# Linear attention: state products one chunk in advance, normed rows turned two levels on, 48 projections in front of the first scores

## The chip, the cores and the metric

The kernel runs on one core of one Trainium2 chip. A core has TensorE (PE, matrix products and transposes into PSUM), VectorE (DVE), ScalarE (ACT), GpSimd (POOL) and SyncE (SP, which issues DMAs); each works through a queue of its own, in order, and waits for the others at semaphores. The metric is the device time of the whole program in microseconds (us), as the median of several runs; lower is better.

## What is computed

One layer on 1024 tokens of width 1024, in fp32: a mixer of two kinds of gated linear attention (four heads with keys of 128, and four heads with keys of 64), an output projection with a norm, and a mixture of 64 experts, two for each token, with a second norm. The change is in the mixer. Cut to what matters:

```python
def chunk_gla(q, k, v, log_g):                       # per head; b = cumulative sum of log_g
    decay = jnp.exp(jnp.where(causal, diff, -jnp.inf))
    scores = jnp.einsum('bhntsk,bhnsk->bhnts', q[..., :, None, :] * decay, k)
    o_intra = jnp.einsum('bhnts,bhnsv->bhntv', scores, v)
    u = jnp.einsum('bhnsk,bhnsv->bhnkv', k * jnp.exp(b_last - b), v)
    def step(S, inp):                                # the running state, chunk after chunk
        g_n, u_n = inp
        return g_n[..., None] * S + u_n, S
    ...
    o_inter = jnp.einsum('bhntk,bhnkv->bhntv', q * jnp.exp(b), s_prev)
    o = o_intra + o_inter

def hybrid_mixer(x, w_in, w_a2, b_a, lb, norm_h, norm_g, w_out):
    hq, hf, hi, hg, gq, gk, gv, ga, gg = jnp.split(x @ w_in, split_at, axis=-1)
    ...
    o_h = head_rms_norm(o_h, norm_h) * jax.nn.silu(hg.astype(jnp.float32))
    ...
    o_g = head_rms_norm(o_g, norm_g) * jax.nn.silu(gg.astype(jnp.float32))
    o = jnp.concatenate([o_h, o_g], axis=-1).astype(x.dtype)
    return o @ w_out
```

The experts' weights, 64 times three matrices of 1024 x 512, are 403 MB; each is read from HBM once.

## The kernel before

**The two parts.** First the mixer with its output projection and the router, then the experts, whose weights stream through SBUF in tiles of 2 MB. The first four of these tiles are loaded while the output projection runs; the rest begins when the router has finished.

**Order.** TensorE's order is the order of the code (`tc.manual_schedule` for PE). The queues of VectorE, ScalarE and GpSimd are put in order by the scheduler of the language, from what the code issues; so a change of TensorE's code also moves instructions on those.

**Projections.** `queue` lists the blocks of `x @ w_in`, each 128 columns wide, with what is done to its result. A block is 48 products of 128 x 512 (L176, L178 and L180: x and the weights are split into a high and a low part of fp32r, three products make one) in two halves of 24; its weights are loaded, cast on ScalarE (L155, `wh`) and subtracted on VectorE (L156, `wl`). `fill(n)` issues the next n products of the queue; the mixer uses them to cover the other work. `to_rows` takes a block of values: ScalarE copies a half to SBUF (L217, `vt`), TensorE transposes it some projections later (L222; `late` holds the count at which), and VectorE copies it to `VOA` (L223). `gated` multiplies `VOA` by a silu gate (L229, L231).

**Units.** `gla(u, ...)` runs for units 0 to 5: units 0 to 3 are one head each, units 4 and 5 two heads of half width. A unit works on chunks of 128 tokens (`NT` = 8). Its scores are made in seven levels: `level` builds decayed keys and queries (GpSimd L471 and L472 subtract cumulative sums, ScalarE L473 takes the exponential, VectorE L436, or L454 with two heads, and L475 multiply into `K2` and `Qb`, two buffers each), `scores` makes the products (TensorE L485, then L500, and L512 or L518), and VectorE masks them into `acc` (L422, L424). For each level: `fill(n_lv)`, one of the turns left by the unit before, then the scores. A turn (L616) transposes half a head of normed rows, which VectorE scales first (L610, after a chain of small operations on the squares' sums, L80 to L88), and VectorE copies the result to `VOA` (L617).

**Chunks.** Behind the levels comes a loop over the chunks. The output of chunk c is q times the running state (L576) plus scores times values (L578); the state's own product (L584) follows, and VectorE updates the state in one of the two tiles `Sg` (L591 copies the first, L593 does the others). ScalarE sums the squares of the output (L598), VectorE copies it to `osb` (L599). Then comes one step of the next unit's preparation (gates, the scans L393, on VectorE, ScalarE and GpSimd), and `fill(n_ch)`. Outputs and state products share the PSUM pool `ps_ou`, three buffers; a new tile gets the buffer that was released first in the program's order. Turns, transposes and scores share `ps_tr`, two buffers.

Of the kernel before, what the change touches and what calls it, by code (L numbers as in the profile page):

```python
# [9 lines left out]
F32 = mybir.dt.float32  # L10
# [4 lines left out]
OP = mybir.AluOpType  # L15
# [5 lines left out]
NT = T // 128  # L21
# [35 lines left out]
def mixer_moe_kernel(ctx: ExitStack, tc: tile.TileContext, x_in, xT_in, wf_in, wv_in, wvg_in, wa2_in,  # L57
# [3 lines left out]
    V, S, G, PE = nc.vector, nc.scalar, nc.gpsimd, nc.tensor  # L61
# [8 lines left out]
    VOA = voap.tile([128, NT, NH, 128], F32, name="VOA")  # L70
# [33 lines left out]
    ps_ou = psA.enter_context(tc.tile_pool(name="ps_ou", bufs=3, space=PSUM))  # L104
# [27 lines left out]
    Sg = [pers.tile([128, 256], F32, name=f"Sg{i}") for i in range(2)]  # L132
# [3 lines left out]
    queue, wts, late = [], {}, []  # L136
    done, count, cur, limit = [0], [0], [None], [0]
# [63 lines left out]
    def fill(n):  # L201
        end = count[0] + n
        while count[0] < end and step():
            pass
# [8 lines left out]
    def to_rows(h):  # L213

        def evac(ps, ts):
            vt = g2.tile([128, 512], F32, name="vt", bufs=1)
            S.copy(vt, ps)  # L217

            def turn():
                tp = ps_tr.tile([128, 4, 128], F32, name="trp")  # L220
                for i in range(4):
                    PE.transpose(tp[:, i], vt[:, i * 128:(i + 1) * 128], ident)  # L222
                V.tensor_copy(VOA[:, ts.start // 128:ts.stop // 128, h], tp)  # L223
            late.append((count[0] + 10, turn))
        return evac

    def gated(h):
# [166 lines left out]
            if c % 2:  # L394
                yield

    def gla(u, n_lv, n_ch, before, during):


        h0, nh, sc = (u, 1, 1.0) if u < 4 else (2 * u - 4, 2, 1.0 / 16.0)  # L400
        q, k, lg, P = ready.pop(u)
        dk = 128 // nh
        W = nh * 128
        Pc = P.rearrange("p (c i) -> p c i", i=128)
        A = Ab
        KLt = g1.tile([128, NT, 128], F32, name="KLt")
# [118 lines left out]
        QI = g1.tile([128, T], F32, name="QI")  # L525
        gdec = small.tile([128, NT], F32, name="gdec")
# [19 lines left out]
            S.copy(KLt[:, half * 4:half * 4 + 4], tp)  # L546

        kqs = {0: level(0)}
        for li in range(7):
            if li < 6:  # L550
                kqs[li + 1] = level(li + 1)
            if li == 2:
                decayed_k()
            if li == 3:
                decayed_q()
            fill(n_lv)
            if before:
                before.pop(0)()
            if li in (5, 6):
                turn_k(li - 5)  # L560
            scores(li, *kqs.pop(li))
# [6 lines left out]
        if u < 5:  # L568
            need(at[f"q{u + 1}"])
        steps = during()  # L570
        Sp = None
        for c in range(NT):
            cs = slice(c * 128, (c + 1) * 128)
            op = ps_ou.tile([128, W], F32, name="ou")
            if c:
                PE.matmul(op, QI[:, cs], Sp[:, :W], start=True, stop=False)  # L576
            for hh in range(nh):
                PE.matmul(op[:, hh * 128:(hh + 1) * 128], A[hh][:, c], VOA[:, c, h0 + hh], start=(c == 0),  # L578
                          stop=(c == 0 or hh == nh - 1))
            if c < NT - 1:  # L580
                up = ps_ou.tile([128, 128], F32, name="ou")
                for hh in range(nh):
                    r = slice(hh * dk, (hh + 1) * dk)
                    PE.matmul(up[r], KLt[:, c, r], VOA[:, c, h0 + hh], start=True, stop=True)  # L584
                gcol = gdec[:, c:c + 1]
                Sn = Sg[c % 2]
                for hh in range(nh):
                    r = slice(hh * dk, (hh + 1) * dk)
                    w = slice(hh * 128, (hh + 1) * 128)
                    if c == 0:  # L590
                        V.tensor_copy(Sn[r, w], up[r])  # L591
                    else:
                        V.scalar_tensor_tensor(Sn[r, w], Sp[r, w], gcol[r], up[r], op0=OP.mult, op1=OP.add)  # L593
                Sp = Sn
            for hh in range(nh):
                w = slice(hh * 128, (hh + 1) * 128)
                junk = small.tile([128, 128], BF, name="junk")
                S.activation(junk, op[:, w], AF.Square, accum_out=ssq[hh][:, c:c + 1])  # L598
                V.tensor_copy(osb[hh][:, c], op[:, w])  # L599
            next(steps, None)  # L600
            fill(n_ch)
# [4 lines left out]
        turns = []  # L606
# [14 lines left out]
    def mixer():  # L621
        limit[0] = at["g6"]
        for i in range(8):
            PE.matmul(zp, zt[:, 0:128], zt, start=True, stop=True)
        first_blocks()
        setup()
        for _ in prepare(0):
            pass
        turns = []
        for u in range(6):  # L630
            turns = gla(u, 18 if u == 0 else 12, 12 if u < 5 else 6, turns, (lambda: prepare(u + 1)) if u < 5 else (lambda: iter(())))
        for t_ in turns:
            t_()
        limit[0] = len(queue)

    with tc.manual_schedule(engines={mybir.EngineType.PE}):
        mixer()
        gl.close()
# [14 lines left out]
    gcol = tb.tile([128, NE // 2], F32, name="gcol")  # L653
# [711 lines left out]
```

## Time and profile before

| | us |
|---|---|
| median of 3 runs | 1620.42 |
| lowest to highest | 1619.65 to 1620.74 |
| the profiled execution | 1625.67 |
| its span, first to last instruction | 1623.8 |
| TensorE busy | 1447.7 |
| VectorE busy | 726.0 |
| ScalarE busy | 404.4 |
| GpSimd busy | 272.0 |

The mean granted clock of TensorE is 0.957 of its full speed. The profile cuts the span into 40 slices of 40.6 us. Slices 0 to 11 are the mixer, 12 to 15 the output projection and the router, 16 to 39 the experts. A busy time says how long an engine works, a list of waits who it waited for, a timeline what stands in its queue and what ended an idle time before an instruction (in square brackets).

### The profile page before, as it was taken

How to read it: one execution, taken by the hardware profiler on the slowest of the kernel's cores; microseconds unless marked ns; L12 is line 12 of the kernel's file. 1: busy time of each engine (PE TensorE's matmuls, PEld its weight loads, DVE VectorE, ACT ScalarE, POOL GpSimd, SP SyncE). 2: the span in 40 equal slices, each digit the busy share in tenths (PEclk: the TensorE clock that was granted, in tenths of full speed). 3: DMA queues.
4: the chain of work that ended last, by engine and by line, in shares of the span. 5: the costliest groups of instructions: out<-in, count | busy, mean ns of one | idle time of the engine just before them, and what ended most of it. 6: DMA issues, size and time to landing. Idle time of an engine off the chain costs nothing. (4 is left out here: it accounts for less than half of the span.)

```text
span 1623.8 us, 22905 instructions
## 1 busy us (share of the span) xinstructions
PE 1447.7 (89%) x9303; PEld 809.3 (50%) x9303; DVE 726.0 (45%) x1842; ACT 404.4 (25%) x749; POOL 272.0 (17%) x228
## 2 busy tenths in 40 slices
PE   7899899999999997999989989989988989988985
PEld 5677677777778775334334333333333433333432
DVE  4656544666856995233323322422422422422424
ACT  5345443435543232211111110110110110110110
POOL 4523231423202552010000000000000000000000
PEclk9899999899999997999999999999999999999998
DMA  4111100010117316999999999999999999999992
GB/s 164 34 33 34 34 27 27 27 41 20 35 46 309 125 61 255 393 425 425 427 425 427 426 425 427 426 426 426 426 427 426 426 426 426 425 427 426 423 393 89
DMA packets 61966, 450.18 MB, mean 277 GB/s; under 512 B 12192, under 2 KB 20640, under 8 KB 36896
## 3 DMA queue, kind: packets, MB, share of 16 engines
q1 hardware_dynamic: 50768, 430.01, 63.8%
q0 software_dynamic: 9216, 12.61, 2.2%
q10 hardware_dynamic: 1872, 6.06, 1.0%
q8 instruction: 74, 1.21, 0.3%
q14 instruction: 36, 0.29, 0.1%
HBM read 448.63 MB, written 20.97 MB: 289 GB/s over the span
## 5 line engine op out<-in xcount | busy, mean ns | idle before, releaser
L1150 PE MATMUL gu<-w2u,VOA 128*64 128x512 f32 x1024 | 253.8, 625 | 49.8 <-DMA w2u<-in_wu_dram 34.6
L1150 PE MATMUL gu<-w1u,VOA 128*64 128x512 f32 x1024 | 258.2, 623 | 36.8 <-DMA w1u<-in_wu_dram 27.6
L1026 DVE TENSOR_TENSOR sg<-sg,gu 128x512 f32<-128x512 f32 x32 | 22.0, 688 | 543.5 <-PE gu L1150 543.5
L1150 PEld LDWEIGHTS gu<-w1u,VOA 128*64 128x64 f32 x1024 | 84.6, 144 | 205.3 <-issue 148.6
L1150 PEld LDWEIGHTS gu<-w2u,VOA 128*64 128x64 f32 x1024 | 80.5, 144 | 213.0 <-issue 143.1
L176 PE MATMUL pp<-xh,wh 128*128 128x512 f32 x416 | 177.7, 427 | 0.0
L178 PE MATMUL pp<-xl,wh 128*128 128x512 f32 x416 | 167.1, 402 | 0.5 <-issue 0.5
L180 PE MATMUL pp<-xh,wl 128*128 128x512 f32 x416 | 167.4, 402 | 0.0
L1009 POOL DMA_INDIRECT out_dram<-VOA,oidx x32 | 32.3, 1008 | 604.9 <-DVE VOA L1051 593.1
L1036 ACT COPY hT<-tp 128x512 f32<-128x512 f32 x32 | 18.8, 586 | 394.1 <-PE tp L1034 394.1
L1176 PE MATMUL yp<-w1u,hT 128*64 128x512 f32 x512 | 116.4, 595 | 0.0
L1176 PE MATMUL yp<-w2u,hT 128*64 128x512 f32 x512 | 113.4, 595 | 0.0
L1042 ACT ACTIVATE y<-yp,gcol 128x512 fp32r<-128x512 f32 x64 | 44.0, 688 | 190.1 <-PE yp L1176 190.1
L176 PEld LDWEIGHTS pp<-xh,wh 128*128 128x128 f32 x416 | 81.0, 195 | 18.6 <-issue 2.4
L180 PEld LDWEIGHTS pp<-xh,wl 128*128 128x128 f32 x416 | 80.5, 194 | 18.6
L178 PEld LDWEIGHTS pp<-xl,wh 128*128 128x128 f32 x416 | 81.2, 195 | 15.0 <-issue 0.8
L471 POOL TENSOR_TENSOR d<-P 128x512 f32<-128x512 f32 x36 | 47.9, 1331 | 229.2 <-DVE Qb L475 152.7
L1043 DVE SCALAR_TENSOR_TENSOR y<-yp,gcol,y 128x512 fp32r<-128x512 f32 x64 | 47.9, 749 | 76.5 <-ACT y L1042 76.3
L1004 POOL DMA_INDIRECT VOA<-x1d,gidx x32 | 32.8, 1024 | 290.2 <-issue 214.3
L1025 ACT ACTIVATE sg<-gu 128x512 f32<-128x512 f32 x32 | 19.1, 597 | 240.0 <-PE gu L1150 240.0
L1108 PE MATMUL cp<-y,same 128*128 128x512 f32 x304 | 78.5, 404 | 0.0
L156 DVE TENSOR_TENSOR wl<-wr,wh 128x512 fp32r<-128x512 f32 x52 | 43.8, 842 | 70.4 <-ACT wh L155 43.8
(276 smaller groups left out, 2087.5 us busy)
## 6 DMA issues: line engine op xcount, KB each, us to landing
w1u<-in_wu_dram SPq DMA_DIRECT2D x32, 2048.0 KB, 29.6
w1u<-in_wd_dram SPq DMA_DIRECT2D x32, 2048.0 KB, 30.6
w2u<-in_wg_dram SPq DMA_DIRECT2D x31, 2048.0 KB, 28.1
w1u<-in_wg_dram SPq DMA_DIRECT2D x30, 2048.0 KB, 29.3
w2u<-in_wd_dram SPq DMA_DIRECT2D x30, 2048.0 KB, 32.1
w2u<-in_wu_dram SPq DMA_DIRECT2D x30, 2048.0 KB, 31.1
wr<-in_wf_dram SPq DMA_DIRECT2D x36, 256.0 KB, 2.6
r<-in_x_dram SPq DMA_DIRECT2D x8, 512.0 KB, 3.5
```

The costliest lines, as they stand in the source:

```text
L156: V.tensor_tensor(lo[:, ks], rs[j], hi[:, ks], OP.subtract)
L176: PE.matmul(ps, hi[:, k], xh[:, k, ts], start=(k == 0), stop=False)
L178: PE.matmul(ps, hi[:, k], xl[:, k, ts], start=False, stop=False)
L180: PE.matmul(ps, lo[:, k], xh[:, k, ts], start=False, stop=(k == KT - 1))
L471: G.tensor_tensor(ev[:, :, 0], ref, Pv[:, :, 0], OP.subtract)
L1004: return G.indirect_dma_start(out=dst, out_offset=None, in_=x1d, in_offset=bass.IndirectOffsetOnAxis(ap=idx, axis=0), bounds_check=T - 1, ...
L1009: return G.indirect_dma_start(out=dst, out_offset=bass.IndirectOffsetOnAxis(ap=idx, axis=0), in_=src, in_offset=None, bounds_check=rows - ...
L1042: S.mul(yh[:, ns], yps[n], gate_col)
L1043: V.scalar_tensor_tensor(yl[:, ns], yps[n], gate_col, yh[:, ns], op0=OP.mult, op1=OP.subtract)
L1108: PE.matmul(cps[n], m, ys[q][:, i, n * 512:(n + 1) * 512], start=(first and j == 0 and i == 0), stop=(last and j == len(ms) - 1 and i == 1))
L1150: PE.matmul(dst[64 * b:64 * b + 64], xt[:, c, 64 * b:64 * b + 64], utile[6 * p + u + b][:, c], start=(c == 0), stop=(c == KT - 1))
L1176: PE.matmul(yps[n][64 * b:64 * b + 64], hT[:, c, 64 * b:64 * b + 64], utile[6 * p + 4 + b][:, c, n * 512:(n + 1) * 512], start=(c == 0), s ...
```

## The change

In `gla`, the state's product and update are taken out of the chunk's code into a function `state(c)`. `state(0)` is issued ahead of the loop, `state(c + 1)` behind the output products of chunk c; chunk c's output uses `states[c - 1]`. The two tiles `Sg` and the three PSUM buffers stay. The turns of the unit before go to levels 2 and 3 (levels 2 to 5 for the four turns of unit 4, which run in unit 5) instead of from level 0 on. `late` holds transposes back for 20 projections instead of 10. A new argument `n_0` puts 48 projections in front of the first scores of unit 0, which then has 12 in front of each level and behind the last, in place of 18; the sum over the unit is 144 in both. Other units have 12 as before and `n_0` = 0.

```diff
@@ to_rows @@
-            late.append((count[0] + 10, turn))
+            late.append((count[0] + 20, turn))
@@ gla @@
-    def gla(u, n_lv, n_ch, before, during):
+    def gla(u, n_0, n_lv, n_ch, before, during):
...
         kqs = {0: level(0)}
+        fill(n_0)
         for li in range(7):
...
             fill(n_lv)
-            if before:
+            if before and li > 1:
                 before.pop(0)()
...
         steps = during()
-        Sp = None
+        states = {}
+
+        def state(c):
+
+            up = ps_ou.tile([128, 128], F32, name="ou")
+            Sn = states[c] = Sg[c % 2]
+            for hh in range(nh):
+                r = slice(hh * dk, (hh + 1) * dk)
+                PE.matmul(up[r], KLt[:, c, r], VOA[:, c, h0 + hh], start=True, stop=True)
+            for hh in range(nh):
+                r = slice(hh * dk, (hh + 1) * dk)
+                w = slice(hh * 128, (hh + 1) * 128)
+                if c == 0:
+                    V.tensor_copy(Sn[r, w], up[r])
+                else:
+                    V.scalar_tensor_tensor(Sn[r, w], states[c - 1][r, w], gdec[:, c:c + 1][r], up[r], op0=OP.mult,
+                                           op1=OP.add)
+
+        state(0)
         for c in range(NT):
             cs = slice(c * 128, (c + 1) * 128)
             op = ps_ou.tile([128, W], F32, name="ou")
             if c:
-                PE.matmul(op, QI[:, cs], Sp[:, :W], start=True, stop=False)
+                PE.matmul(op, QI[:, cs], states[c - 1][:, :W], start=True, stop=False)
             for hh in range(nh):
                 PE.matmul(op[:, hh * 128:(hh + 1) * 128], A[hh][:, c], VOA[:, c, h0 + hh], start=(c == 0),
                           stop=(c == 0 or hh == nh - 1))
-            if c < NT - 1:
-                up = ps_ou.tile([128, 128], F32, name="ou")
...
-                Sp = Sn
+            if c < NT - 2:
+                state(c + 1)
@@ mixer @@
-            turns = gla(u, 18 if u == 0 else 12, 12 if u < 5 else 6, turns, (lambda: prepare(u + 1)) if u < 5 else (lambda: iter(())))
+            turns = gla(u, 48 if u == 0 else 0, 12, 12 if u < 5 else 6, turns, (lambda: prepare(u + 1)) if u < 5 else (lambda: iter(())))
```

The lines move by six in what follows: the output's product with the state is L595 in the change, with the scores L597, the state's product L580, its copy and updates L585 and L587, the copy to `osb` L605, the turn L622 and its copy L623.

First, VectorE's queue at the start of unit 1's chunks. `Sg` are the state's tiles, `osb` holds the chunks' outputs, `Qb` and `K2` belong to the next unit's level 0, `wl` is a weight split. Before:

```order
L156 TENSOR_TENSOR wl_1504<-wr_1505,wh_1503 128x512
L591 COPY Sg0_118<-ou_1493 128x128
L599 COPY osb_1489<-ou_1491 128x128
L462 TENSOR_TENSOR Qb0_114<-q_1178,d_1723 128x512
L463 TENSOR_TENSOR Qb0_114<-q_1178,d_1723 128x512
L436 TENSOR_TENSOR K20_112<-k_1177,d_1723 128x512 x2
L593 SCALAR_TENSOR_TENSOR Sg1_119<-Sg0_118,gdec_1076,ou_1529 128x128
L599 COPY osb_1489<-ou_1526 128x128
```

and in the change:

```order
L585 COPY Sg0_118<-ou_1491 128x128
L156 TENSOR_TENSOR wl_1507<-wr_1508,wh_1506 128x512
L587 SCALAR_TENSOR_TENSOR Sg1_119<-Sg0_118,gdec_1076,ou_1496 128x128
L605 COPY osb_1489<-ou_1494 128x128
L462 TENSOR_TENSOR Qb0_114<-q_1172,d_1723 128x512
L463 TENSOR_TENSOR Qb0_114<-q_1172,d_1723 128x512
L436 TENSOR_TENSOR K20_112<-k_1171,d_1723 128x512 x2
L587 SCALAR_TENSOR_TENSOR Sg0_118<-Sg1_119,gdec_1076,ou_1532 128x128
L605 COPY osb_1489<-ou_1529 128x128
```

The first copy of the state has gone ahead of the weight split, the update of state 1 ahead of `Qb` and `K2`, and the update of state 2 stands where that of state 1 stood.

Second, ScalarE's queue in unit 0's levels: `d` is a level's exponential, `vt` the copy of a half of projected values, `wh` the cast of weights.

```order
 L538 ACTIVATE lg<-lg 128x1024
-L473 ACTIVATE d<-d 128x1024 x2
-L217 COPY vt<-pp 128x512
-L155 CAST wh<-wr 128x512
-L473 ACTIVATE d<-d 128x1024
-L155 CAST wh<-wr 128x512
-L217 COPY vt<-pp 128x512
-L473 ACTIVATE d<-d 128x1024
-L155 CAST wh<-wr 128x512
+L473 ACTIVATE d<-d 128x1024
+L217 COPY vt<-pp 128x512
+L473 ACTIVATE d<-d 128x1024
```

The first copy to `vt` stands behind one exponential (level 2) instead of two (levels 2 and 3).

Third, VectorE's queue at the end of unit 5's levels. `acc` takes the masked scores, `K2` and `Qb` with `d_4548` (`d_4542` in the change) are the last level's, the three next rows prepare the router. Before:

```order
L424 COPY_PREDICATED acc_4045<-mski_107,trp_4474 128x512
L454 TENSOR_TENSOR K21_113<-k_3252,d_4548 64x8x2x32
L475 TENSOR_TENSOR Qb1_115<-q_3253,d_4548 128x8x64
L647 CAST trib_4915<-cst_63 128x128
L648 MEMSET oneb_4916 128x128
L649 MEMSET msum_4914 128x64
L231 TENSOR_TENSOR VOA_65<-VOA_65,pp_4461 128x4x128
```

and in the change:

```order
L424 COPY_PREDICATED acc_4045<-mski_107,trp_4468 128x512
L454 TENSOR_TENSOR K21_113<-k_3246,d_4542 64x8x2x32
L475 TENSOR_TENSOR Qb1_115<-q_3247,d_4542 128x8x64
L653 CAST trib_4915<-cst_63 128x128
L654 MEMSET oneb_4916 128x128
L655 MEMSET msum_4914 128x64
L623 TENSOR_SCALAR VOA_65<-trp_4563,cols_64 128x4x128
L231 TENSOR_TENSOR VOA_65<-VOA_65,pp_4449 128x4x128
```

The copy of the last turn (L623), which stood four levels earlier, now follows the last level's queries.

## Rows read from the trace of the kernel before

**Rows 1.** The page's 40 slices: what the DMAs moved, GB/s

```profile
GB/s 164 34 33 34 34 27 27 27 41 20 35 46 309 125 61 255 393 425 425 427 425 427 426 425 427 426 426 426 426 427 426 426 426 426 425 427 426 423 393 89
```

**Rows 2.** TensorE's waits, 0 to 500 us: total us, times, longest

```profile
PE trp L616 <- DVE osb L610: 13.0, 6, 3.2
PE trp L222 <- ACT vt L217: 9.4, 4, 7.0
PE ou L576 <- DVE Sg L593: 8.3, 4, 3.2
...
PE ou L576 <- DVE Sg L591: 3.4, 2, 2.0
```

**Rows 3.** TensorE's timeline, unit 0: start, us, line, operation, [idle before]

```profile
42.49 0.76 PE L485 MATMUL trp<-Qb,K 128*32 128x32 f32 x64 [0.95 <-DVE K L436]
...
46.51 0.39 PE L180 MATMUL pp<-xh,wl 128*128 128x512 f32 x1
53.93 1.11 PE L222 MATMUL trp<-cst,vt 128*128 128x128 f32 x4 [7.03 <-ACT vt L217]
```

**Rows 4.** ScalarE's timeline, unit 0

```profile
36.80 1.28 ACT L460 ACT_TABLE_LOAD   x1
...
49.34 1.06 ACT L473 ACTIVATE d<-d 128x1024 f32<-128x1024 f32 x1 [2.06 <-POOL d L472]
...
53.31 0.57 ACT L217 COPY vt<-pp 128x512 f32<-128x512 f32 x1
```

**Rows 5.** Stretches: us, busy PE, PEld, DVE, ACT, POOL, PEclk, DMA share, GB/s

```profile
49.20:59.50 10.30, 5.57 (x76) 4.35 (x77) 10.03 (x12) 4.17 (x5) 6.08 (x5) 0.50 0.15 48
189.20:196.00 6.80, 5.72 (x77) 2.95 (x78) 3.91 (x6) 1.28 (x1) 1.78 (x2) 0.50 0.14 41
237.00:240.40 3.40, 3.40 (x9) 2.64 (x8) 2.56 (x5) 1.40 (x4) 3.20 (x3) 0.50 0.15 56
267.70:274.50 6.80, 5.72 (x77) 4.60 (x78) 3.91 (x6) 1.28 (x1) 1.79 (x2) 0.50 0.14 41
318.90:325.70 6.80, 5.77 (x18) 4.80 (x19) 6.12 (x9) 2.37 (x6) 5.30 (x4) 0.50 0.01 2
...
421.30:424.70 3.40, 3.32 (x133) 2.92 (x134) 2.81 (x10) 0.00 (x0) 0.00 (x0) 0.50 0.27 81
416.00:446.00 30.00, 26.88 (x737) 21.88 (x740) 27.57 (x62) 13.64 (x19) 8.59 (x8) 0.94 0.12 39
```

**Rows 6.** TensorE's timeline, first turns in units 2 and 5

```profile
190.28 1.09 PE L616 MATMUL trp<-cst,osb 128*128 128x128 f32 x4 [3.17 <-DVE osb L610]
...
421.38 1.11 PE L616 MATMUL trp<-cst,osb 128*128 128x128 f32 x4 [3.12 <-DVE osb L610]
```

**Rows 7.** VectorE's timeline, the chunks of unit 1: updates of the state

```profile
161.04 0.34 DVE L593 SCALAR_TENSOR_TENSOR Sg<-Sg,gdec,ou 128x128 f32<-128x128 f32 x1
...
166.13 0.34 DVE L593 SCALAR_TENSOR_TENSOR Sg<-Sg,gdec,ou 128x128 f32<-128x128 f32 x1
```

**Rows 8.** TensorE's timeline, chunks that wait in units 2, 3 and 4

```profile
235.78 0.49 PE L576 MATMUL ou<-Sg,QI 128*128 128x128 f32 x2 [2.02 <-DVE Sg L591]
...
319.93 0.80 PE L576 MATMUL ou<-Sg,QI 128*128 128x128 f32 x2 [3.17 <-DVE Sg L593]
...
397.03 0.86 PE L576 MATMUL ou<-Sg,QI 128*128 128x256 f32 x2 [2.49 <-DVE Sg L593]
```

**Rows 9.** VectorE's timeline, the chunks of units 2 and 3

```profile
234.84 0.69 DVE L156 TENSOR_TENSOR wl<-wr,wh 128x512 fp32r<-128x512 f32 x1
...
317.99 0.69 DVE L223 COPY VOA<-trp 128x512 f32<-128x512 f32 x1
...
319.54 0.33 DVE L593 SCALAR_TENSOR_TENSOR Sg<-Sg,gdec,ou 128x128 f32<-128x128 f32 x1
```

**Rows 10.** VectorE's and TensorE's timelines, end of unit 5's levels

```profile
445.24 0.77 DVE L475 TENSOR_TENSOR Qb<-q,d 128x512 f32<-128x512 f32 x1
...
445.92 0.82 PE L500 MATMUL trp<-Qb,K 128*32 128x32 f32 x64
```

More of the change, by code (lines that the diff above doesn't have):

```diff
@@ L579, in gla @@
                           stop=(c == 0 or hh == nh - 1))
-            if c < NT - 1:
-                up = ps_ou.tile([128, 128], F32, name="ou")
[L582 to L593, printed above, removed]
-                Sp = Sn
+            if c < NT - 2:
+                state(c + 1)
             for hh in range(nh):
```

## The prediction

> **What bounds the kernel now.** I read the slices first, then TensorE's list of waits, then the timelines of the engines named there, and last the busy times of the stretches at half clock. The kernel has two parts. From about 640 us on, the experts' weights stream at 425 GB/s without a break [rows 1]; nothing in the change touches that part, and all of it starts when the mixer and the router are done. The mixer (0 to 488 us) runs on TensorE, in the order of the code, and that is where the change is. So a microsecond taken from the mixer is a microsecond taken from the total: the reader is to see in [rows 1] that the DMAs have little to do between 528 and 609 us (125 and 61 GB/s), and thus no transfer holds the router back.
>
> In the mixer TensorE waits 34.1 us in three kinds of places [rows 2]: for normed rows that VectorE has not scaled yet (L616, 13.0 us in 6 waits), for a copy of projected values on ScalarE before they are transposed (L222, 9.4 in 4), and for the running state that VectorE updates (L576, 8.3 and 3.4). The second price is the clock: behind the longer waits TensorE is granted 0.50, 1.2 instead of 2.4 GHz [rows 5]. A stretch at 0.50 loses half of its busy time: 2.8 us at 49.2, 2.9 at 189.2, 1.7 at 237.0, 2.9 at 267.7, 2.9 at 318.9, 1.7 at 421.3.
>
> **Part 1, unit 0 (48 projections in front of its first scores, transposes 20 projections behind their copy instead of 10).** Before, 34 projections and the first scores are issued by 46.90 (46.51 + 0.39), with a wait of 0.95; then the transposes wait 7.03 for ScalarE's copy [rows 3]. A projection takes 0.228: 16 of them fill the 3.65 us from the end of the scores at 43.25 to 46.90. Now 44 projections come first and no scores: 46.90 - 1.71 + 10 x 0.228 = 47.5. ScalarE's copy (0.57) stood behind the exponentials of levels 2 and 3 and ran at 53.31 [rows 4]; it now stands behind level 2's alone (second excerpt of the order), which ends at 50.40 [rows 4] because GpSimd feeds it, and nothing on GpSimd changes its order. So the copy ends at 51.0 and the wait is 3.5 instead of 7.98: 4.5 us less. The clock still falls, since 3.5 is as long as the waits that cost two of the stretches in [rows 5]; I count no gain there. Two things come back. Six projections (1.4 us) that stood between the last scores and the first chunk now stand earlier, while VectorE's work for the chunks is tied to those last scores; TensorE therefore arrives 1.4 us too early and waits. And transposes that lay in a stretch which waits for VectorE anyway now lie behind it, 0.6. Left: 2.5 us (bounds: 0, if the first chunks wait longer still, and 7.3, if the clock holds and the 2.8 are won too). ScalarE also loads its table two more times in this unit (1.28 each in [rows 4]); the exponentials they delay are those of levels 5 and 6, needed some 5 us later, so I cost them at nothing; without that cover they would cost 2.6.
>
> **Part 2, the normed rows two levels on.** A turn needs VectorE's scaling of the whole unit and stands in front of the level's scores, so these scores wait with it. Two levels are 24 projections (5.5 us) and two sets of scores, against waits of at most 3.2; the scores that are first now were prepared during the chunks. In units 2 and 3 the waits of 3.17 [rows 6] and 3.2 (the longest of [rows 2]) go, and with them the half clock at 189.2 and 267.7, 2.9 each [rows 5]: 12.1. Of the 6 waits the one of unit 5 is below; the three others share 3.5, and one of these, at the mixer's end, isn't moved: 2.3 for units 1 and 4. Together 14.4 (bounds: 2 us, where VectorE is the bound there too, and 15).
>
> Unit 5 has two heads and four turns, and is different. Its wait was 3.12, and 1.7 for the clock. But VectorE is busy for 27.6 of the 30 us from 416 to 446 [rows 5]. It finishes the keys and queries of the last level at 446.01, and the scores of level 5 run at 445.92 beside that [rows 10]. The fourth turn now stands right in front of these scores, and its copy out of PSUM is on VectorE behind that same last query product (third excerpt of the order); the scores need the PSUM buffer of this turn. VectorE's 27.6 us are not less, so the scores can start at most 2.4 us earlier, and going through the queue row by row I find them at 445.7. With what ScalarE has left behind them I take 0.6 us (bounds: -1.5 and 4.8).
>
> **Part 3, the state's products one chunk in advance.** This is meant for the 11.7 us of L576, and I don't expect it to remove them. Before, chunk c's first product needs the update of state c-1, whose own product was issued one chunk earlier. Now it needs nothing that is late; but in the same chunk the product of state c+1 is issued, and of the three PSUM buffers it gets the one that the update of state c frees. That update's product, too, was issued one chunk earlier. On VectorE the update of state c stands where that of c-1 stood (first excerpt of the order). In unit 1 VectorE is at the places of [rows 7]: behind Qb and K of the next unit at 161.04 and behind lg at 166.13. TensorE waited for the end of the first, 161.38; now it waits there with one product (0.45 us) already issued, and a later update is waited for at the second place. VectorE has one update (0.34) more ahead of each place, and a set of transposes (0.6) comes later: unit 1 loses 0.3 (bounds: -2, and 3.8 if all its waits go). The 2.4 us that L222 waited outside unit 0's levels lie in the same stretches of units 0 to 2; holding the transposes back longer removes these waits, and VectorE's place takes the time, so they are in these figures.
>
> In unit 2 the wait of 2.02 is for the state's first copy [rows 8], behind a weight split of 0.69 [rows 9]. The copy now stands ahead of the split, so the wait is 1.3 and another of 0.5 follows for the next update; the 1.7 of half clock behind it goes with a chance of about 6 in 10. Gain 1.3 (0.2 to 4). In unit 3 the wait of 3.17 [rows 8] ends with an update at 319.54, ahead of which VectorE copied turned rows for 0.69 [rows 9]; that copy is later now. The product waits until some 319.4, with 0.45 of work issued before: wait 2.3, half clock in about half of the cases; further on VectorE is the bound again. Gain 2.1 (0.5 to 6). In unit 4 the wait of 2.49 [rows 8] shrinks to 0.8, but VectorE's next update is as late as before and takes most of it back: 0.8 (-0.5 to 4). Sum of part 3: 3.9.
>
> **Sum.** 2.5 + 14.4 + 0.6 + 3.9 = 21.4 us. The profiled execution took 1625.67 (span 1623.8), 5.3 more than the median of 1620.42; taken from that execution the sum gives 1604.3, from the median 1599.0, which I predict.
>
> **Rivals.** (A) Part 3 does what it says: the state is ready, the buffer too. For it speaks that the product which the chunk waits for is really two chunks old; against it that VectorE's backlog is the cause and isn't smaller. Then the waits of [rows 2] go except 1.2 at the mixer's end and 3.5 in the first unit, 29.4, with the clock of 237.0, 318.9, 397 (1.7, as at 421.3), 189.2 and 267.7, 12.1, less some 3 for unit 5: 38.5, or 1582. (B) VectorE binds units 2 and 3 as it binds unit 5: the turn goes, but scores wait for masks and keys, which now stand in front of the scaling. Against it: VectorE is busy for 3.91 of the 6.80 us from 189.2 [rows 5]. Then part 2 gives 2.3 and the total 9.3: 1611. (C) On the other side: the extra product in flight makes every chunk wait for a buffer. Its place is the product of state c+1 in chunks 1 to 5 of six units, 30 places; it decides once the update of a state lags its product by more than the chunk's 12 projections, 2.7 us. With 1.3 us each, the mean wait of those that stand under 2 us in [rows 2] (11.7 less 3.17, 2.49 and 2.02 is 4.0 for three), that is 39 us; less what parts 1 and 2 save, 17.5, it is 21.5 us slower: 1642. Against it: before, TensorE waited for the state's update in 6 of 42 chunks [rows 2]. The Trainium skill (Perfetto Trace Analysis, section Optimization Strategy) speaks for C: it says that the same gap repeating on the engine that should be saturated can mean there isn't enough SBUF or PSUM for the next tile to be allocated. By that rule the change, which keeps one product more in the same three buffers, comes out at 1642; the trace of before doesn't bear it out, as the waits of [rows 8] end with the update of the state and not with a copy that frees a buffer. (D) The gain of part 2 is taken back by new falls of the clock, whose place shifts with every microsecond won: 6 stretches of 2.9 would do it, and leave 4 us or less: no change.
>
> **How the numbers follow.** Forecast 0.68 (own range 1591 to 1607), A 0.11, B 0.14, C 0.03, D 0.04. The range leaves out A, C and D: 1586 to 1612. A measurement of this kernel can tell about 0.2% (3.2 us) from no change; faster by more has 0.93, within it 0.04, slower 0.03.
>
> **What would show it.** Right, if in the changed kernel's list of waits the turns wait for nothing in units 1 to 4 and the clock stays at full in the first levels of units 2 and 3; if the first transposes wait 3 to 4 us near 47; if the waits of L576 come back at the new product of the state (L580), ended by VectorE's update, some 8 to 12 us in all; and if unit 5's scores of level 5 wait for VectorE. Wrong, if L580 and L576 both wait nothing (A), or if scores (L485) wait in units 1 to 4 (B).

## The result, and the profile after

The changed kernel takes **1601.18 us** (median of 4 runs, 1600.37 to 1601.88) against 1620.58 for the kernel before (4 runs, 1619.65 to 1621.54): ratio 0.9866, 95% interval 0.9845 to 0.9886. That is 19.4 us faster; 1599.0 was predicted, with 1586 to 1612 as the range. Its profiled execution took 1601.88 (span 1600.1), that of before 1625.67 (1623.8). So the two spans stand 23.7 us apart where the medians stand 19.4 apart: the profiled execution of before was a long one.

TensorE's waits from 0 to 500 us (total us, times, longest), to be held against [rows 2]. L580 is the state's product, L595 the chunk's product with the state (L576 before), L622 the turn (L616 before).

```profile
PE ou L580 <- DVE Sg L587: 13.7, 11, 1.8
...
PE trp L222 <- ACT vt L217: 4.3, 2, 3.7
...
PE pp L383 <- DVE lg L385: 2.0, 2, 1.4
PE trp L500 <- DVE VOA L623: 2.0, 1, 2.0
PE trp L622 <- DVE osb L616: 1.3, 1, 1.3
PE trp L485 <- DVE acc L424: 1.3, 2, 0.8
PE ou L595 <- DVE Sg L585: 1.2, 1, 1.2
```

The turns waited 13.0 us in six places; now 1.3 in one, at the mixer's end. The transposes (L222) fell from 9.4 to 4.3. The state's waits did not fall: 8.3 and 3.4 before, 13.7 and 1.2 now. But no single one is longer than 1.8 us, where 2.0, 2.49 and 3.17 stood [rows 8]. What that did is in the stretches (columns as in [rows 5]; of after, then three short ones of before that [rows 5] does not hold):

```profile
50.00:56.80 6.80, 5.50 (x15) 4.54 (x16) 5.71 (x6) 3.29 (x5) 3.00 (x2) 0.50 0.08 27
182.80:189.60 6.80, 6.80 (x152) 3.42 (x152) 6.66 (x17) 2.63 (x4) 3.69 (x2) 1.00 0.20 63
253.00:259.80 6.80, 6.80 (x151) 5.47 (x151) 6.66 (x17) 2.49 (x3) 3.65 (x2) 1.00 0.21 65
225.00:229.00 4.00, 3.70 (x18) 3.04 (x19) 3.22 (x8) 0.61 (x2) 1.56 (x2) 1.00 0.21 68
300.90:307.70 6.80, 5.55 (x27) 4.46 (x27) 4.82 (x7) 1.78 (x2) 5.36 (x4) 1.00 0.00 0
357.20:360.60 3.40, 3.40 (x9) 2.62 (x8) 1.01 (x2) 3.37 (x4) 0.00 (x0) 0.50 0.06 13
```

```profile
301.80:305.20 3.40, 3.40 (x10) 2.63 (x9) 1.18 (x2) 3.34 (x5) 0.00 (x0) 0.50 0.03 7
376.90:380.30 3.40, 3.40 (x9) 2.62 (x9) 1.29 (x3) 3.34 (x5) 0.00 (x0) 0.50 0.00 1
397.40:400.80 3.40, 3.40 (x14) 2.47 (x13) 3.26 (x4) 2.39 (x7) 1.98 (x3) 0.50 0.00 0
```

From unit 0's first transposes to the mixer's end, before had nine stretches at half clock (0.50), the changed kernel has two. The first levels of units 2 and 3 (182.8, 253.0) run at full clock and without a gap, and the chunks behind the state's waits (225.0, 300.9) at full clock too. Of the two that are left, that at 50.0 follows the wait of the first transposes, and that at 357.2 stands where 376.9 stood before, behind the same instruction of unit 4's chunks (L383).

Where the time went, by the starts of TensorE's rows. A unit's levels run from the last product with the values of the unit ahead (L597, L578 before) to the first product of its own chunks (L580 or L597); its chunks run from there to the last. The start of the first expert product is 23.97 us earlier (636.51 to 612.54).

| stretch | before, us | after, us | difference | the prediction's term |
|---|---|---|---|---|
| unit 0, levels and chunks | 117.30 | 114.24 | -3.06 | -2.5 |
| levels of units 1 and 4 | 73.30 | 72.02 | -1.28 | -2.3 |
| levels of units 2 and 3 | 87.47 | 75.82 | -11.65 | -12.1 |
| unit 5's levels | 42.87 | 41.13 | -1.74 | -0.6 |
| chunks of unit 1 | 29.77 | 29.41 | -0.36 | +0.3 |
| chunks of unit 2 | 29.42 | 26.97 | -2.45 | -1.3 |
| chunks of unit 3 | 36.07 | 33.86 | -2.21 | -2.1 |
| chunks of unit 4 | 39.20 | 37.64 | -1.56 | -0.8 |
| chunks of unit 5, last turns | 32.14 | 31.84 | -0.30 | 0 |
| mixer, to its last turn | 487.54 | 462.93 | -24.61 | -21.4 |

Read alone, this table says that every step was about right. The experiments say otherwise.

### The profile page after: what moved, and what is told of

Its sections match the earlier page's. It is cut to its first block, busy times and chain, and to the rows that moved or that the text cites. A ratio compares the mean times of both kernels' runs of the same rounds, so it can differ in the third digit from the quotient of the medians.

```text
span 1600.1 us, 22873 instructions
## 1 busy us (share of the span) xinstructions
PE 1442.8 (90%) x9303; PEld 798.1 (50%) x9303; DVE 730.9 (46%) x1842; ACT 408.1 (26%) x752; POOL 276.8 (17%) x228
## 5 line engine op out<-in xcount | busy, mean ns | idle before, releaser
L1156 PE MATMUL gu<-w2u,VOA 128*64 128x512 f32 x1024 | 261.3, 639 | 45.4 <-DMA w2u<-in_wu_dram 28.4
L176 PE MATMUL pp<-xh,wh 128*128 128x512 f32 x416 | 173.1, 416 | 0.0
L471 POOL TENSOR_TENSOR d<-P 128x512 f32<-128x512 f32 x36 | 51.6, 1433 | 202.3 <-DVE ny L88 65.3
L178 PEld LDWEIGHTS pp<-xl,wh 128*128 128x128 f32 x416 | 79.3, 191 | 13.7
L1114 PEld LDWEIGHTS cp<-y,same 128*128 128x128 f32 x304 | 54.7, 188 | 35.5 <-issue 25.2
## 6 DMA issues: line engine op xcount, KB each, us to landing
w1u<-in_wu_dram SPq DMA_DIRECT2D x32, 2048.0 KB, 29.5
```

The source lines that it names most:

```text
L176: PE.matmul(ps, hi[:, k], xh[:, k, ts], start=(k == 0), stop=False)
L178: PE.matmul(ps, hi[:, k], xl[:, k, ts], start=False, stop=False)
L471: G.tensor_tensor(ev[:, :, 0], ref, Pv[:, :, 0], OP.subtract)
L1114: PE.matmul(cps[n], m, ys[q][:, i, n * 512:(n + 1) * 512], start=(first and j == 0 and i == 0), stop=(last and j == len(ms) - 1 and i == 1))
L1156: PE.matmul(dst[64 * b:64 * b + 64], xt[:, c, 64 * b:64 * b + 64], utile[6 * p + u + b][:, c], start=(c == 0), stop=(c == KT - 1))
```

## The experiments

All medians in one place; the ratio is to the kernel before, run on the same chip (1623.07, 1623.21 or 1625.74 us there). Of runs that stand in different rows the times are compared, since the changed kernel came out at 1601.2 and 1601.3 while before moved by 5. It was not run beside the 1625.74; four kernels were (transposes +10, both pools, unit 5's turns, the last two together), so these are held against a changed kernel that was measured on another occasion.

| kernel | median us (lowest to highest, runs) | ratio, 95% interval |
|---|---|---|
| part 1 alone | 1622.60 (1621.03 to 1625.23, 11) | 1.0000, 0.9989 to 1.0010 |
| part 2 alone | 1611.44 (1609.91 to 1612.04, 5) | 0.9934, 0.9920 to 0.9947 |
| part 3 alone | 1623.67 (1620.22 to 1625.79, 11) | 1.0007, 0.9997 to 1.0018 |
| changed, again | 1601.29 (1601.26 to 1601.41, 4) | 0.9862, 0.9842 to 0.9881 |
| changed without part 3 | 1607.38 (1605.28 to 1608.74, 5) | 0.9894, 0.9877 to 0.9912 |
| changed without part 1 | 1608.90 (1607.88 to 1611.23, 5) | 0.9910, 0.9893 to 0.9928 |
| changed, transposes +10 | 1609.23 (1608.49 to 1612.32, 6) | 0.9899, 0.9881 to 0.9918 |
| state's product in the other pool | 1599.18 (1596.08 to 1600.02, 5) | 0.9850, 0.9833 to 0.9867 |
| state's product in both pools | 1596.70 (1595.22 to 1598.10, 5) | 0.9822, 0.9800 to 0.9843 |
| unit 5's turns one level on | 1600.16 (1599.32 to 1600.72, 5) | 0.9845, 0.9824 to 0.9866 |
| the last two together | 1596.35 (1593.17 to 1598.16, 5) | 0.9817, 0.9793 to 0.9840 |

**The kernel before, profiled again.** No edit.

> The kernel before, profiled a second time. The profiled execution on which the sum was made took 5.3 us more than the median and shows half clock in nine stretches of the mixer. Theory: some of these come and go from execution to execution (the short ones behind waits near 1 us, at 301.8, 376.9 and 397.4 us), so this one takes about 1620 us and shows six or seven. Rival: the clock falls at the same nine places in every execution and the 5 us lie in the expert part, behind 640 us.

It took 1626.92 us: both profiled executions of before lie in the upper part of what its runs take (1620 to 1629 over all its runs). The clock falls at the same nine places, so the theory missed; the rival was right in that and wrong in the rest, since the expert part does not vary either (969.8 and 969.6 us from its first product to its last). What varies in the mixer is how long a stretch is:

```profile
190.30:193.70 3.40, 3.40 (x10) 1.16 (x9) 1.42 (x3) 1.28 (x1) 1.83 (x2) 0.50 0.28 82
193.70:197.10 3.40, 3.40 (x79) 1.94 (x78) 2.12 (x4) 1.67 (x3) 0.27 (x1) 1.00 0.00 0
395.10:398.50 3.40, 3.19 (x11) 2.40 (x12) 3.21 (x6) 1.82 (x5) 1.98 (x3) 0.50 0.02 5
398.50:401.90 3.40, 3.40 (x9) 2.57 (x8) 3.29 (x5) 1.42 (x5) 2.70 (x2) 0.50 0.00 0
```

Behind unit 2's first turn half clock lasted 6.8 us in [rows 5] and 3.4 here, and unit 2's levels took 49.07 and 48.18; behind unit 4's wait it was 3.4 and now 6.8, and these chunks took 39.20 and 40.80. So one place is worth 0.9 to 1.6 us more or less from execution to execution. Nine such places may be why before scatters over 9 us and the changed kernel, with two, over 1.5; this was not shown. In these two executions the differences cancel: the mixer's last turn starts at 487.54 in both, and the second is longer by 1.4 us between there and the first expert product (150.34 and 148.97).

**Part 1 alone.**

```diff
-            late.append((count[0] + 10, turn))
+            late.append((count[0] + 20, turn))
         kqs = {0: level(0)}
+        fill(n_0)
-            turns = gla(u, 18 if u == 0 else 12, 12 if u < 5 else 6, ...
+            turns = gla(u, 48 if u == 0 else 0, 12, 12 if u < 5 else 6, ...
```

> The kernel before with part 1 alone (48 projections in front of unit 0's first scores, transposes 20 projections behind their copy; the chunks and the turns as before). Theory of the prediction: 2.5 us for unit 0, so 1618.1 us, with a wait of 3.7 at the first transposes near 47.6, the clock falling behind it, and the waits of 2.4 us at transposes in the chunks of units 0 to 2 gone but taken back by the state's product. Rival: the 3.1 us that unit 0 gained in the changed kernel came from the chunks (part 3), and part 1 alone gives 0: 1620.6.

No change. TensorE's waits (L577 is the chunk's product with the state, L617 the turn):

```profile
PE ou L577 <- DVE Sg L594: 14.3, 11, 2.4
PE trp L617 <- DVE osb L611: 14.1, 6, 3.2
...
PE ou L577 <- DVE Sg L592: 4.9, 3, 2.0
...
PE trp L222 <- ACT vt L217: 3.7, 2, 3.5
```

The transposes lost 5.7 us of waiting ([rows 2]: 9.4), the state's product gained 7.5 (19.2 instead of 11.7), and the turns 1.1. The prediction's sentence that VectorE's place takes back what the transposes no longer wait is right in this kernel. The levels of unit 0 are shorter than in either profile of before (82.6 us against 88.5 and 86.9), and in this execution, one of the shortest of its eleven (1621.11), the mixer ends 3.9 us earlier than in the profiled ones of before. Over all runs nothing of it is seen: the interval leaves at most 1.8 us. So the rival's number came without the rival's reason.

**Part 2 alone.**

```diff
-            if before:
+            if before and li > 1:
                 before.pop(0)()
```

> The kernel before with part 2 alone (the normed rows turned two levels on). Theory of the prediction: 14.4 us for units 1 to 4 and 0.6 for unit 5, so 1605.6 us; full clock in the first levels of units 2 and 3, no wait of a turn except at the mixer's end, the state's waits of 2.02 and 3.17 us in units 2 and 3 still there with the clock falling behind them. Rival (falls of the clock shift): half of the clock's gain goes to new stretches, 1611. Rival (part 2 carries all of the result, the others nothing): 1601.2.

11.6 us by the medians (8.6 to 13.0 by the interval), not 15. The waits are as expected, and the state's two long ones stay:

```profile
PE ou L576 <- DVE Sg L593: 10.1, 5, 3.2
...
PE ou L576 <- DVE Sg L591: 3.5, 2, 2.1
...
PE trp L616 <- DVE osb L610: 1.3, 1, 1.3
```

The levels of units 2 and 3 take 43.24 and 32.53 us, 5.8 and 5.9 less than in the profile of before, as the sum had it; unit 5's levels 42.90, nothing less. There the half clock behind the first turn (421.3 in [rows 5]) is gone, but one came at another place of the same levels, behind 1.99 us in which TensorE was idle and the profile names nothing that it waited for:

```profile
417.10:420.50 3.40, 3.40 (x9) 2.65 (x8) 1.92 (x3) 1.06 (x1) 1.98 (x3) 0.50 0.02 5
```

So of the 7.5 us that the clock cost behind the turns of units 2, 3 and 5 (2.9, 2.9 and 1.7), 1.7 went to a new stretch: the rival that names 1611 has the number and a small part of the reason. The difference between 14.7 us in the traces (the last turn starts at 472.81) and 11.6 is about what the profiled execution of before (1625.67) stands above the median on this chip (1623.07).

**Part 3 alone.** The diff of the change from `states = {}` to `state(c + 1)`, on the kernel before.

> The kernel before with part 3 alone (the state's product one chunk in advance). Theory of the prediction: the wait moves from the chunk's first product to the new state's product, 3.9 us in all from units 2, 3 and 4 and nothing from unit 1, so 1616.7 us. Rival: in the changed kernel the chunks gained 0.6, 2.7, 2.4 and 2.0 us in units 1 to 4, 7.7 together, and that was all part 3: 1612.9. Rival: what part 3 gains is lost at the turns, which wait for VectorE's scaling as late as before: within 1 us of 1620.6.

No change: the last rival. The waits (L622 is the turn):

```profile
PE trp L622 <- DVE osb L616: 14.6, 6, 4.8
PE trp L222 <- ACT vt L217: 13.5, 5, 7.0
PE ou L580 <- DVE Sg L587: 9.9, 6, 3.2
```

The state's waits are 11.2 with L595's 1.3, as long as before; the transposes wait 4.1 us more, the turns 1.6 more (unit 5's first one 4.8 instead of 3.12). TensorE comes earlier to two other kinds of waits. In this execution, the shortest of the eleven (1620.22), the mixer still ends 4.9 us earlier than in the profiled ones of before; over all runs nothing of it is seen.

**Leaving one part out.** The changed kernel again, and with one part as before.

> The changed kernel a second time, beside the kernels that leave one part out. Theory: as in its first runs, a ratio of 0.987 to the kernel before, and the same waits: 12 to 15 us at the state's new product, 3.7 at unit 0's first transposes, 2.0 at unit 5's scores of level 5, none at the turns except 1.3 at the mixer's end. Rival: the half clock at 357 us comes and goes, and with it some 1.7 us.

> The changed kernel without part 3 (the state's product stands where it stood before; 48 projections first and the turns two levels on). Theory of the prediction: part 3 is worth 3.9 us, so 3.9 slower than the changed kernel. Theory that the single parts suggest (what the chunks win is lost at the turns while these wait for VectorE, and is kept once they don't): part 3, which alone gave nothing, is worth 6 to 8 here, the sum of what the chunks of units 2 to 5 won in the changed kernel. Rival: VectorE binds anyway, part 3 is worth nothing, 0 to 1 slower.

> The changed kernel without part 1 (18 projections per level in unit 0, transposes 10 projections behind their copy; the turns two levels on and the state's product in advance). Theory of the prediction: part 1 is worth 2.5 us, so 2.5 slower than the changed kernel. Theory that the single parts suggest: alone it gave nothing because the first turns took it back; with these moved its 3 us stay. Rival: its 3 us are taken back by the wait of the state's product in the chunks of units 0 and 1, which ends when VectorE gets there: 0 to 1 slower.

The first is as before (1601.29). Without part 3 it is 6.1 us slower, without part 1 it is 7.6: the theory that what the parts win is kept once the turns are moved, and more of part 1 than that theory said. Parts 1 and 3 that gave nothing alone give 10.1 on top of part 2 (1611.44 to 1601.29). One at a time on top of part 2 they give 4.1 (part 1, 1607.38) and 2.5 (part 3, 1608.90, with ranges that overlap). So a good part comes with the turns alone; what comes only with both is 3.5 us by these medians and 1.3 by the ratios. Without part 1 the waits are

```profile
PE trp L222 <- ACT vt L217: 13.5, 5, 7.0
PE ou L580 <- DVE Sg L587: 9.8, 6, 3.2
```

and one of them, in unit 2's chunks (timeline: start, us, operation, idle time before and what ended it):

```profile
237.89 0.33 PE L222 MATMUL trp<-cst,vt 128*128 128x128 f32 x1 [2.25 <-ACT vt L217]
```

The chunks of unit 2 show it best. They take 29.4 before, 29.5 with part 2 or 3 alone, 29.0 with part 1 alone, 29.1 without part 3, 29.5 without part 1, and 27.0 in the changed kernel. Without part 3 the state is waited for (2.15 us, and half clock behind it); without part 1, with the state ready, TensorE comes 2.25 us too early for ScalarE's copy. Only with both does neither stop it.

The kernel without part 3 has these waits for the state (L577 is the chunk's product with the state) and these stretches at half clock behind unit 0, besides one at 359.7 that the changed kernel has too (357.2):

```profile
PE ou L577 <- DVE Sg L594: 12.6, 11, 1.9
...
PE ou L577 <- DVE Sg L592: 5.0, 3, 2.1
```

```profile
226.50:229.90 3.40, 3.40 (x12) 2.82 (x11) 2.48 (x5) 0.89 (x3) 2.42 (x2) 0.51 0.25 80
298.20:301.60 3.40, 3.40 (x12) 2.72 (x11) 3.37 (x3) 1.11 (x2) 3.32 (x2) 0.50 0.00 0
427.90:431.30 3.40, 3.40 (x10) 2.63 (x9) 0.36 (x1) 2.19 (x9) 0.00 (x0) 0.51 0.02 5
```

**Which half of part 1.**

```diff
-            late.append((count[0] + 20, turn))
+            late.append((count[0] + 10, turn))
```

> The changed kernel with the transposes of projected values 10 projections behind their copy, as before, instead of 20; the 48 projections in front stay. Without all of part 1 the changed kernel was 7.6 us slower, and its transposes waited 13.5 us in 5 places, 6.4 of them in the chunks of units 0 to 2 and 4. Theory: these waits belong to the 10 projections, so 3 to 5 us slower than the changed kernel, with 2.4 in unit 2's chunks, and the first transposes of unit 0 wait some 6 us instead of 3.7 with the same end. Theory of the prediction (held back or not, VectorE's place takes the time): 0 to 1 slower, and the rest of the 7.6 lies with the 48 projections.

7.9 us slower, as much as without all of part 1. So the 20 projections behind the copy are worth 6 to 8 us here (6.0 by the ratios), and of the 48 projections in front nothing is to be seen in the total (0.3 us the other way, 1.8 for them by the ratios, both inside the scatter). In the traces they do shorten unit 0, from 118.17 us without all of part 1 to 115.29; unit 2's chunks then take 1.5 more (29.50 and 31.04), and have a stretch at half clock at 235.3 that the other execution lacks. Whether they are worth nothing or the 2.5 forecast stays open. The waits:

```profile
PE trp L222 <- ACT vt L217: 12.5, 5, 6.1
PE ou L580 <- DVE Sg L587: 9.9, 7, 3.2
```

6.11 us of L222 are unit 0's first transposes, as expected; the rest lies in the chunks of units 0, 1, 2 and 4. More was lost than the 3 to 5 us expected, 4.1 of it in unit 2's chunks instead of 2.4: behind unit 0 the clock fell four times to the middle of unit 5 (235.3, 307.0, 361.6, 412.8), against once in the changed kernel.

**The state's PSUM buffer.** In the changed kernel the product of state c+1 and the update of state c use the same PSUM buffer.

```diff
-            up = ps_ou.tile([128, 128], F32, name="ou")
+            up = ps_tr.tile([128, 128], F32, name="trp")
```

> The changed kernel, with the state's product in the PSUM buffers of the transposes (two, in turn) instead of the three that it shares with the chunk's output. There the product of state c+1 always gets the buffer that the update of state c has just left; now it needs the update of c-1 only, and so does the chunk's output. Theory that the buffer makes the wait: of the 13.7 us at the state's product some 11 go (3.2 in each of units 0 and 1, 3 in unit 3, 2 in unit 4; worked out from the ends of VectorE's updates in the changed kernel and one chunk, 3.4 us, between two products), and 8 to 11 us of the total. Theory that VectorE's place is what counts: the waits come back at the chunk's output or at the next scores, 0 to 2 us faster. Rival on the other side: the transposes of the projected values now wait for VectorE's updates, up to 2 us slower.

2.1 us faster. The waits at the state's product nearly go, but the transposes share these buffers now:

```profile
PE trp L222 <- DVE Sg L587: 4.5, 2, 2.3
PE trp L580 <- DVE Sg L587: 3.0, 2, 1.9
...
PE trp L485 <- DVE acc L424: 2.0, 1, 2.0
```

That left it open whether a buffer or VectorE's place makes the transposes' two waits of 2.27 us. With every second product in the other pool, a transpose buffer stays free:

```diff
-            up = ps_ou.tile([128, 128], F32, name="ou")
+            up = (ps_tr.tile([128, 128], F32, name="trp") if c % 2
+                  else ps_ou.tile([128, 128], F32, name="ou"))
```

> The changed kernel, with every second product of the state in a PSUM buffer of the transposes, so that one transpose buffer stays free. With all of them there the waits at the state's product fell from 13.7 to 3.0 us, but the transposes of projected values waited 2.27 us twice for VectorE's updates, and the kernel won 2.1 us. Theory that the buffer makes the wait: now the chunks of units 0 and 1 win some 3 us each (1.83 before), unit 4's 1.4; unit 5 gives 1.2 back as there; 5 to 6 us faster than the changed kernel, 1595 to 1596. Theory that VectorE's place decides: the chunk's output waits for the updates at the same times as the transposes did, and the kernel takes 1599 as with the other buffers.

4.6 us faster than the changed kernel, near the theory of the buffer. No wait for an update of the state is left but one of 1.2 at the first state:

```profile
PE trp L222 <- ACT vt L217: 10.4, 4, 4.2
...
PE trp L500 <- DVE VOA L623: 1.9, 1, 1.9
...
PE ou L595 <- DVE osb L605: 1.4, 1, 1.4
...
PE ou L595 <- DVE Sg L585: 1.2, 1, 1.2
```

The chunks of units 0 and 1 take 26.5 us, 2.9 less than in the changed kernel, each. So the buffer makes the waits at the state's product. That 13.7 us of them are worth only 4.6 is because others grew: the transposes wait 10.4 instead of 4.3, the chunk's output 1.4 for the copy to `osb`. Unit 3's chunks lose 1.3 (a transpose that waits 4.19 us for ScalarE's copy), and unit 5's levels 1.9, where 1.2 was expected. Most of the 1.9 is the clock: behind the same wait of 1.95 us at the scores of level 5, TensorE was granted 0.50 here and 1.00 in the changed kernel (first row this kernel, second the changed one):

```profile
416.20:419.60 3.40, 3.40 (x70) 2.86 (x71) 0.69 (x1) 3.28 (x11) 0.00 (x0) 0.50 0.02 5
```

```profile
422.30:425.70 3.40, 3.32 (x75) 2.85 (x76) 0.71 (x2) 3.28 (x11) 0.01 (x1) 1.00 0.02 5
```

**Unit 5's turns at levels 1 to 4.**

```diff
-            if before and li > 1:
+            if before and li > (0 if u == 5 else 1):
```

> The changed kernel with unit 5's four turns at levels 1 to 4 instead of 2 to 5, so that no turn stands in front of the scores of level 5. Theory of the prediction (VectorE is the bound of this unit, the turn's copy only the last piece in its queue): the 1.7 to 2.0 us at the scores of level 5 become a wait for the last keys and queries, which VectorE ends 1.1 us earlier than the fourth turn's copy; 0.3 to 1.1 us faster, within 0.1 per cent. Rival (the turn's place alone makes the wait): all of it goes, 2 us. Rival on the other side: the first turn waits for VectorE's scaling, 3.1 us and 1.7 of half clock, as in the kernel before.

1.1 us below the changed kernel by the medians, 0.07%, no more than could be chance, and not from this unit: its levels take 41.07 us, 41.13 in the changed kernel. The wait of 2.0 at the scores of level 5 is gone, and one of 1.36 stands at level 6, for ScalarE's copy of the level-5 scores:

```profile
423.58 0.32 PE L518 MATMUL trp<-Qb,K 128*128 128x64 f32 x1 [1.36 <-ACT Ab L505]
```

As the prediction had it, the unit is bound by what feeds it and not by the turn's place, though the last wait is now one for ScalarE and not for VectorE's keys and queries; the first turn did not wait for VectorE's scaling.

> The two before together: the state's products in two pools' buffers and unit 5's turns at levels 1 to 4. Theory that the buffer makes the wait: 6 us faster than the changed kernel, 1595, since unit 5 doesn't take its part back. Theory that VectorE's place decides: 1598 to 1599, and unit 5's scores wait as much longer as TensorE comes earlier.

1596.35 us, the fastest of all: 5 us under the changed kernel, but nothing that can be told from the state's buffers alone (1596.70). Unit 5's levels go from 43.07 with the buffers alone to 41.58, without the half clock that stood there.

## Why the prediction was right, and where not

**The bound** was right: the experts take 969.8 us in both kernels, and the mixer's microseconds are the total's.

**Part 1** was mis-sized: the half of it that was put at nothing carries most. The first transposes do what was foreseen:

```profile
51.30 1.12 PE L222 MATMUL trp<-cst,vt 128*128 128x128 f32 x4 [3.71 <-ACT vt L217]
```

TensorE comes at 47.59 (47.5 forecast), resumes at 51.30 (51.0), and waits 3.71 (3.5). The 2.5 us that I put down to unit 0 are there in the traces (2.9 less with the 48 projections) but don't stand clear of the scatter in the time, while the 20 projections, which I valued at nothing outside unit 0, are worth 6 to 8. The failed sentence is "holding the transposes back longer removes these waits, and VectorE's place takes the time". It holds in the kernel before, as part 1 alone shows, and for the most part without part 3 (the transposes wait 4.0 us there and 9.5 with part 2 alone, the state 17.6 and 13.6). I carried it over to a kernel in which part 3 makes the state ready earlier.

**Part 2** was right in its mechanism: no turn waits in units 1 to 4, and the first levels of units 2 and 3 are at full clock. The term was too large: 15.0 in the sum, 11.6 measured alone. The stretches were read from an execution that took 5.3 us more than the median, and the sum was then taken from the median. I said how the two stand to each other, but did not ask which of the sum's terms that execution had too much of. The half clock of 6.8 us behind unit 2's turn, 3.4 in the second profile, is one, and the new stretch at 417.1 another piece. **Unit 5** came out as described, by a wait for VectorE right behind the fourth turn's copy:

```profile
421.65 0.68 DVE L623 TENSOR_SCALAR VOA<-trp,cols 128x512 f32<-128x512 f32 x1
```

```profile
422.38 0.71 PE L500 MATMUL trp<-Qb,K 128*32 128x32 f32 x54 [1.95 <-DVE VOA L623]
```

The gain there, 0 with part 2 alone (where the new stretch stands) and 1.7 in the changed kernel's trace, lies around the 0.6 forecast.

**Part 3** was right in its mechanism, too: the waits came back at L580, ended by the update of the state. One of eleven, in unit 1, TensorE's row and VectorE's:

```profile
157.58 0.49 PE L580 MATMUL ou<-VOA,KLt 128*128 128x128 f32 x2 [1.25 <-DVE Sg L587]
```

```profile
157.19 0.34 DVE L587 SCALAR_TENSOR_TENSOR Sg<-Sg,gdec,ou 128x128 f32<-128x128 f32 x1
```

They sum to 14.9 instead of 8 to 12, in shorter pieces than before, and yet the term was too small: 6.1 instead of 3.9, given the other parts, and 0 without. By TensorE's timelines the chunks of units 1 to 5 wait 14.0 us, 13.0 before (both with L222 and L383), and yet are 6.9 shorter. Four stretches of half clock went there (237.0, 301.8, 318.9, 397.4: 1.7 each, and 2.9 for the long one), and that of 376.9 stayed (357.2): 8.0 by the price used in the prediction (half of the busy time at half clock), less 1.0 of longer waits, 7.0. Against the kernel without part 3, the nearer one, three such stretches went, 5.1 by that price, and the state's waits fell from 17.6 to 14.9, while the mixer is 6.3 shorter (469.21 and 462.93). That the clock carries most of part 3 here is worked out from these rows, not tried apart.

**The sum** of 21.4 stands against 19.4 in the result, and against 21.9 on the chip of the second runs (1623.21 and 1601.29). It came out by luck, as two errors cancel: part 2 some 3 us too large, parts 1 and 3 together 6.4 where 10.1 was measured. The terms were added as if independent. Parts 1 and 3 show nothing while the turns wait, 4.1 and 2.5 one at a time once these are moved, and 10 together.

**The rivals.** A did not happen, but its world exists: with buffers of a second pool the state's waits do go, for 4.6 us, not for the 17 between A and the forecast. B: no turn's place was taken by VectorE in units 2 and 3; the two waits of L485 for `acc` lie in unit 5. C: I turned the Trainium skill's rule away (Perfetto Trace Analysis, section Optimization Strategy: the same gap repeating on the engine that should be saturated can mean too little SBUF or PSUM for the next tile). Its price was far off, since 13.7 us came at eleven places and not 39 at thirty. But the trace of the changed kernel now shows the repeating gap, and another PSUM buffer removed it: by that rule the place was named rightly. D: no new falls in the changed kernel, as the one at 357.2 stands where that of 376.9 stood; with part 2 alone there was one (417.1).

## What to carry to other kernels

Where one engine's stream meets several others, an edit that removes one wait may show nothing until the next wait behind it is gone as well; so test parts by leaving one out of the whole, not only by adding one to the start. When a product is issued earlier, follow the buffer that it writes: if it is the one that the late consumer still reads, the wait only changes its name. And before a sum made from one profiled execution is taken from a median, profile a second time, and price the places that differ between the two at their shorter length; here that takes 1.2 us (2.9 to 1.7) off a term that was some 3 us too large.

## What was not expected of the hardware

The clock is not a function of the wait alone. At the same place, after the same wait for ScalarE's copy (3.71 and 3.67 us), TensorE was granted half clock (1.2 GHz) for 6.8 us in one execution of the changed kernel (50.0 to 56.8, above) and full clock (2.4 GHz) in another:

```profile
49.30:56.10 6.80, 5.47 (x86) 4.45 (x87) 5.76 (x6) 3.33 (x5) 3.01 (x2) 1.00 0.08 28
```

The scores of level 5 are a second such place (1.95 us of waiting, then 0.50 or 1.00, above). And a wait of 1.39 us in front of small products (L383, on 16 partitions) is followed by half clock in both executions (357.2 and 356.0), as one of 0.79 at the same place was before (376.9), though not with part 1 alone, while waits of 1.57 and 1.76 in unit 3's chunks are not (behind the second, 1.00 in the stretch from 300.90, above):

```profile
355.79 0.48 PE L383 MATMUL pp<-gaT,wa 16*128 16x256 f32 x1 [1.39 <-DVE lg L385]
```

```profile
300.97 0.49 PE L580 MATMUL ou<-VOA,KLt 128*128 128x128 f32 x2 [1.76 <-DVE Sg L587]
```

Stretches at half clock came as 3.4 or 6.8 us at one and the same place.
